# A contrast kernel: the first four tiles loaded through two queues, and the first store in one piece

## The chip, the cores and the metric

The kernel runs on one core of one Trainium2 chip. The metric is the time of one execution on the device in microseconds (us). Three runs of the kernel before gave 238.89, 239.13 and 239.41 us; the median, 239.13 us, is the time that the change is compared with.

## The reference

The input `x` is 16 x 3 images of 512 x 512 pixels in fp32, 50.33 MB, and the output has the same shape. Each image is pulled away from its own mean by a factor of 1.5 and clipped:

```python
mean = np.mean(x, axis=(2, 3), keepdims=True)
return np.clip(mean + factor * (x - mean), 0, 1).astype(np.float32)
```

## The kernel before

The input is taken as one flat array and cut into 12 tiles of 128 rows with 8192 numbers each: 32 KB in each of the 128 partitions, 4 MB a tile. An image fills 32 rows, so a tile holds four whole images, and each tile can be finished on its own.

The tiles pass through a ring of six buffers in SBUF (`BUFS = 6`); tile t lives in buffer t % 6 and is changed in place. The order is written out by hand in the last block of the function (L103 to L112): the loads of tiles 0 to 5 are issued at the start, then for each tile `compute(t)` runs, followed by the load of tile t + 6, which goes into the buffer that tile t leaves. That load can't be issued before tile t has been stored.

All loads (`load`, L68 to L76) go through SP's queue, which the profile calls q1. Tile 0 comes in two pieces, 2048 columns (`SHORT`) and then 6144; tile 1 comes whole; tiles 2 and 3 are one DMA, and so are tiles 4 and 5. All stores (`store`, L100 and L101) go through ScalarE's queue, q10 in the profile. A queue's DMAs are worked off in its own order, by 16 DMA engines that serve both queues.

For one tile, `compute` does the following. VectorE adds up the first 4352 columns (`SUM`) of each row (L81), while ScalarE adds up the other 3840 with an ACTIVATE (L84). TensorE multiplies the two columns of sums by a block matrix (L86, L87), which gives every row of an image the shift (1 - factor) x mean in PSUM. VectorE then computes factor x + shift (L91) and clips (L94), both over the whole tile in place, and ScalarE issues the store. For tile 0 alone the two steps L91 and L94 and the store are done in two parts (`FIRST`), 2048 columns and then 6144, so that the first store can be issued early.

ScalarE works in program order: a store that waits for L94 stands ahead of the ACTIVATE of the next tile.

Of the kernel before, what the change touches and what calls it, by code (L numbers as in the profile page):

```python
# [1 line left out]

# [4 lines left out]


P = 128  # L10
ROW = 8192
BUFS = 6
SHORT = 2048
FIRST = (SHORT, ROW - SHORT)
SUM = 4352


@with_exitstack
def kernel(
    ctx: ExitStack,  # L20
    tc: tile.TileContext,
    x: bass.AP,
    factor: float,
    out: bass.AP,
):

    nc = tc.nc
    f32 = mybir.dt.float32  # L30
    Alu = mybir.AluOpType
    Act = mybir.ActivationFunctionType

    B, C, H, W = x.shape
    n_img, n_pix = B * C, H * W
    ppi = n_pix // ROW
    per_tile = P // ppi
    n_tiles = n_img // per_tile
    assert ppi * ROW == n_pix and per_tile * n_tiles == n_img

    factor = float(factor)
    wconst = (1.0 - factor) / float(n_pix)

    x_f = x.rearrange("b c h w -> (b c h w)")
    out_f = out.rearrange("b c h w -> (b c h w)")

    def dram(ap, t, c0=0, c1=ROW):
        return bass.AP(tensor=ap.tensor, offset=t * P * ROW + c0, ap=[[ROW, P], [1, c1 - c0]])

    consts = ctx.enter_context(tc.tile_pool(name="consts", bufs=1))  # L50
    xpool = ctx.enter_context(tc.tile_pool(name="xpool", bufs=1))
    small = ctx.enter_context(tc.tile_pool(name="small", bufs=1))
    psum = ctx.enter_context(tc.tile_pool(name="psum", bufs=1, space=bass.MemoryType.PSUM))


    sums = small.tile([P, 2 * n_tiles], f32, name="sums")
    junk = small.tile([P, ROW - SUM], f32, name="junk")
    bias = psum.tile([P, n_tiles], f32, name="bias")

    blockw = consts.tile([P, P], f32, name="blockw")  # L60
    nc.gpsimd.memset(blockw, 0.0)  # L61
    for a in range(0, P, ppi):
        nc.gpsimd.memset(blockw[a : a + ppi, a : a + ppi], wconst)  # L63


    ring = xpool.tile([P, BUFS, ROW], f32, name="ring")

    def load(t, c0=0, c1=ROW, n=1):  # L68

        b = t % BUFS  # L70
        src = bass.AP(
            tensor=x_f.tensor,
            offset=t * P * ROW + c0,
            ap=[[ROW, P], [P * ROW, n], [1, c1 - c0]],
        )
        nc.sync.dma_start(out=ring[:, b : b + n, c0:c1], in_=src)  # L76

    def compute(t):
        xt = ring[:, t % BUFS, :]
        own = sums[:, 2 * t : 2 * t + 2]  # L80
        nc.vector.tensor_reduce(  # L81
            out=own[:, 0:1], in_=xt[:, 0:SUM], axis=mybir.AxisListType.X, op=Alu.add
        )
        nc.scalar.activation(out=junk, in_=xt[:, SUM:ROW], func=Act.Copy, accum_out=own[:, 1:2])  # L84
        shift = bias[:, t : t + 1]
        nc.tensor.matmul(shift, blockw, own[:, 1:2], start=True, stop=False)  # L86
        nc.tensor.matmul(shift, blockw, own[:, 0:1], start=False, stop=True)  # L87
        c = 0
        for n in FIRST if t == 0 else [ROW]:
            part = xt[:, c : c + n]  # L90
            nc.vector.tensor_scalar(  # L91
                out=part, in0=part, scalar1=factor, scalar2=shift, op0=Alu.mult, op1=Alu.add
            )
            nc.vector.tensor_scalar(  # L94
                out=part, in0=part, scalar1=0.0, scalar2=1.0, op0=Alu.max, op1=Alu.min
            )
            store(t, c, c + n)
            c += n

    def store(t, c0, c1):  # L100
        nc.scalar.dma_start(out=dram(out_f, t, c0, c1), in_=ring[:, t % BUFS, c0:c1])  # L101

    with tc.manual_schedule():  # L103
        load(0, c1=SHORT)
        load(0, c0=SHORT)
        load(1)
        load(2, n=2)
        load(4, n=2)
        for t in range(n_tiles):
            compute(t)  # L110
            if t + BUFS < n_tiles:
                load(t + BUFS)  # L112


# [1 line left out]
_INS = ['x', 'factor']  # L116
_OUTS = [((16, 3, 512, 512), 'float32')]

_NUMBERS = {'factor': 1.5}


# [26 lines left out]
```

## Time and profile before

| what | value |
|---|---|
| median of three runs | 239.13 us |
| span of the profiled execution, first to last instruction | 237.3 us |
| VectorE busy | 163.1 us in 38 instructions |
| ScalarE busy | 43.2 us in 25 instructions |
| TensorE busy | 14.1 us in 48 matmuls |
| bytes moved | 50.33 MB read, 50.33 MB written |

The span runs from the first to the last instruction of one profiled execution. No other time is recorded for that execution; the median of the unprofiled runs lies 1.8 us above its span. The strips of the page cut the span into 40 equal slices of 5.93 us; a digit is the busy share in tenths, 9 meaning nine tenths or more. In the list of groups, the numbers behind the first bar are the busy time and the mean duration in ns, and behind the second bar the idle time just before, with what ended it. The windows view gives the same for stretches that one chooses: busy time of each engine, the clock of TensorE, the share of the DMA engines and their rate in GB/s. In a timeline, the first two numbers are start and duration in us.

### The profile page before, as it was taken

Reading aid. Unit: us, or ns where it says so; the run is one execution under the profiler, and the core shown is the slowest. Engines: PE = TensorE matmul, PEld = TensorE weight load, DVE = VectorE, ACT = ScalarE, POOL = GpSimd, SP = SyncE. Lnnn points to the kernel's source line nnn. Section 1 sums busy time; section 2 is a strip of 40 time slices with the busy share of each in tenths; the row PEclk is TensorE's granted clock in tenths of the full one; section 3 lists DMA queues with packets and bytes.
Section 4 is the critical chain, followed back from the end, with each engine's and each line's share of the span. In section 5 each row is a group of like instructions: output and inputs, shape, how many; then the busy total and the mean of one; then the engine's idle time right before and its main releaser. Section 6 shows DMA issues by size and latency. Waiting matters only on the chain.

```text
span 237.3 us, 285 instructions
## 1 busy us (share of the span) xinstructions
PE 14.1 (6%) x48; PEld 12.0 (5%) x48; DVE 163.1 (69%) x38; ACT 43.2 (18%) x25; POOL 0.9 (0%) x9
## 2 busy tenths in 40 slices
PE   0010010001010001010010100100100100010000
PEld 0010010001010001010010100100100100010000
DVE  0079989048989328999989898891892795687000
ACT  2050230041050023050320504101400500500000
POOL 1000000000000000000000000000000000000000
DMA  7999999999999999999999999999999999999996
GB/s 297 410 442 442 421 442 359 456 439 441 442 436 414 403 431 442 442 442 442 436 442 436 414 409 425 442 442 442 442 436 442 436 420 403 425 442 442 442 442 265
DMA packets 3712, 100.66 MB, mean 424 GB/s; under 512 B 384, under 2 KB 384, under 8 KB 384
## 3 DMA queue, kind: packets, MB, share of 16 engines
q1 hardware_dynamic: 1840, 50.33, 49.7%
q10 hardware_dynamic: 1872, 50.33, 49.2%
HBM read 50.33 MB, written 50.33 MB: 424 GB/s over the span
## 4 chain that ended last, share of the span: by engine, by line
DMA 57%; DVE 29%; another core or an unknown queue 3%; PE 1%; SPq 1%; issue 0%; DVEq 0%
DMA ring<-in_x_dram 41%; DMA out_dram<-ring 16%; DVE sums L81 10%; DVE ring L91 9%; DVE ring L94 9%; PE bias L87 1%; SPq L76 1%; DVEq L91 0%
## 5 line engine op out<-in xcount | busy, mean ns | idle before, releaser
L81 DVE TENSOR_REDUCE sums<-ring 128x1 f32<-128x4352 f32 x12 | 56.2, 4683 | 45.7 <-DMA ring<-in_x_dram 45.7
L84 ACT ACTIVATE junk<-ring 128x3840 f32<-128x3840 f32 x12 | 40.8, 3403 | 163.3 <-DMA ring<-in_x_dram 107.5
L91 DVE TENSOR_SCALAR ring<-ring,bias 128x8192 f32<-128x8192 f32 (+2 forms) x13 | 54.1, 4163 | 8.9 <-PE bias L87 7.4
L94 DVE TENSOR_SCALAR ring<-ring 128x8192 f32<-128x8192 f32 (+2 forms) x13 | 53.3, 4099 | 0.4
L86 PE MATMUL bias<-sums,blockw 128*128 128x1 f32 x24 | 7.0, 361 | 190.8 <-ACT junk L84 190.8
L86 PEld LDWEIGHTS bias<-sums,blockw 128*128 128x128 f32 x24 | 6.0, 312 | 191.7 <-ACT junk L84 175.2
L87 PE MATMUL bias<-sums,blockw 128*128 128x1 f32 x24 | 7.0, 363 | 4.3 <-DVE sums L81 3.9
L87 PEld LDWEIGHTS bias<-sums,blockw 128*128 128x128 f32 x24 | 6.0, 311 | 5.3 <-DVE sums L81 5.0
L84 ACT ACTIVATION_READ_ACCUMULATOR junk<-ring 128x1 f32 x12 | 2.2, 186 | 0.0
L84 ACT ACT_TABLE_LOAD x1 | 1.3, 1283 | 0.7 <-PEq L129 0.7
L63 POOL MEMSET blockw<- 32x32 f32 x4 | 0.5, 117 | 0.2
L61 POOL MEMSET blockw<- 128x128 f32 x1 | 0.2, 204 | 0.3 <-POOLq L129 0.3
L129 POOL MEMSET const-bfloat16-1.0<- 128x1 bf16 x1 | 0.1, 111 | 0.0
L129 POOL MEMSET const-uint8-127<- 128x1 uint8 x1 | 0.1, 111 | 0.0
L129 POOL MEMSET const-float32-1.0<- 128x1 f32 x1 | 0.1, 108 | 0.0
L129 POOL MEMSET const-float32-0.0<- 128x1 f32 x1 | 0.1, 103 | 0.2 <-issue 0.2
## 6 DMA issues: line engine op xcount, KB each, us to landing
out_dram<-ring ACTq DMA_DIRECT2D x11, 4096.0 KB, 35.8
ring<-in_x_dram SPq DMA_DIRECT2D x7, 4096.0 KB, 49.7
ring<-in_x_dram SPq DMA_DIRECT2D x2, 8192.0 KB, 66.7
ring<-in_x_dram SPq DMA_DIRECT2D x1, 3072.0 KB, 11.7
out_dram<-ring ACTq DMA_DIRECT2D x1, 3072.0 KB, 28.2
ring<-in_x_dram SPq DMA_DIRECT2D x1, 1024.0 KB, 4.8
out_dram<-ring ACTq DMA_DIRECT2D x1, 1024.0 KB, 17.5
```

Of the source, the lines that this page charges most:

```text
L61: nc.gpsimd.memset(blockw, 0.0)
L63: nc.gpsimd.memset(blockw[a : a + ppi, a : a + ppi], wconst)
L76: nc.sync.dma_start(out=ring[:, b : b + n, c0:c1], in_=src)
L81: nc.vector.tensor_reduce(out=own[:, 0:1], in_=xt[:, 0:SUM], axis=mybir.AxisListType.X, op=Alu.add)
L84: nc.scalar.activation(out=junk, in_=xt[:, SUM:ROW], func=Act.Copy, accum_out=own[:, 1:2])
L86: nc.tensor.matmul(shift, blockw, own[:, 1:2], start=True, stop=False)
L87: nc.tensor.matmul(shift, blockw, own[:, 0:1], start=False, stop=True)
L91: nc.vector.tensor_scalar(out=part, in0=part, scalar1=factor, scalar2=shift, op0=Alu.mult, op1=Alu.add)
L94: nc.vector.tensor_scalar(out=part, in0=part, scalar1=0.0, scalar2=1.0, op0=Alu.max, op1=Alu.min)
L129: nc = _bacc.Bacc("TRN2", target_bir_lowering=False, num_devices=1)
```

## The change

The first four tiles are shared out between the two queues. SP's queue loads tile 0 (in two pieces, as before) and tile 2; ScalarE's queue loads tile 1, now in two pieces as well, and tile 3, and these three DMAs are issued ahead of everything else that ScalarE issues. Tiles 4 and 5 stay one DMA on SP's queue, and so do the later loads, one tile each. The stores stay on ScalarE's queue, behind those three loads. Tile 0 is no longer done in two parts: L91, L94 and the store take the whole tile, as for all others.

```diff
-FIRST = (SHORT, ROW - SHORT)
...
-    def load(t, c0=0, c1=ROW, n=1):
+    def load(t, c0=0, c1=ROW, n=1, queue=nc.sync):
...
-        nc.sync.dma_start(out=ring[:, b : b + n, c0:c1], in_=src)
+        queue.dma_start(out=ring[:, b : b + n, c0:c1], in_=src)
...
-        c = 0
-        for n in FIRST if t == 0 else [ROW]:
-            part = xt[:, c : c + n]
-            nc.vector.tensor_scalar(
-                out=part, in0=part, scalar1=factor, scalar2=shift, op0=Alu.mult, op1=Alu.add
-            )
-            nc.vector.tensor_scalar(
-                out=part, in0=part, scalar1=0.0, scalar2=1.0, op0=Alu.max, op1=Alu.min
-            )
-            store(t, c, c + n)
-            c += n
-
-    def store(t, c0, c1):
-        nc.scalar.dma_start(out=dram(out_f, t, c0, c1), in_=ring[:, t % BUFS, c0:c1])
+        nc.vector.tensor_scalar(
+            out=xt, in0=xt, scalar1=factor, scalar2=shift, op0=Alu.mult, op1=Alu.add
+        )
+        nc.vector.tensor_scalar(
+            out=xt, in0=xt, scalar1=0.0, scalar2=1.0, op0=Alu.max, op1=Alu.min
+        )
+        nc.scalar.dma_start(out=dram(out_f, t), in_=xt)
 
     with tc.manual_schedule():
         load(0, c1=SHORT)
+        load(1, c1=SHORT, queue=nc.scalar)
         load(0, c0=SHORT)
-        load(1)
-        load(2, n=2)
+        load(1, c0=SHORT, queue=nc.scalar)
+        load(2)
+        load(3, queue=nc.scalar)
         load(4, n=2)
         for t in range(n_tiles):
             compute(t)
```

## The prediction

> **What bounds the kernel now.** I read the page first for which resource is full, then the timeline of VectorE for the pace, then the windows for the places where that resource falls short of its own pace.
>
> ```profile
> span 237.3 us, 285 instructions
> ...
> DMA  7999999999999999999999999999999999999996
> GB/s 297 410 442 442 421 442 359 456 439 441 442 436 414 403 431 442 442 442 442 436 442 436 414 409 425 442 442 442 442 436 442 436 420 403 425 442 442 442 442 265
> ...
> q1 hardware_dynamic: 1840, 50.33, 49.7%
> q10 hardware_dynamic: 1872, 50.33, 49.2%
> HBM read 50.33 MB, written 50.33 MB: 424 GB/s over the span
> ...
> L81 DVE TENSOR_REDUCE sums<-ring 128x1 f32<-128x4352 f32 x12 | 56.2, 4683 | 45.7 <-DMA ring<-in_x_dram 45.7
> ```
>
> The DMA engines are at nine tenths or more in 38 of 40 slices: q1 (SP's loads) and q10 (ScalarE's stores) each carry 50.33 MB through the same 16 engines. VectorE, the busiest engine, waits 45.7 us for loads. The first and last slice are the unavoidable ends. The steady pace is the distance between two late tiles:
>
> ```profile
> 184.40 4.68 DVE L81 TENSOR_REDUCE sums<-ring 128x1 f32<-128x4352 f32 x1 [4.99 <-DMA ring<-in_x_dram]
> 189.82 4.49 DVE L91 TENSOR_SCALAR ring<-ring,bias 128x8192 f32<-128x8192 f32 x1 [0.74 <-PE bias L87]
> 194.35 4.43 DVE L94 TENSOR_SCALAR ring<-ring 128x8192 f32<-128x8192 f32 x1
> 203.76 4.69 DVE L81 TENSOR_REDUCE sums<-ring 128x1 f32<-128x4352 f32 x1 [4.98 <-DMA ring<-in_x_dram]
> ```
>
> 203.76 - 184.40 = 19.36 us, in which one tile is loaded and one stored: 8.389 MB / 19.36 us = 433 GB/s. VectorE needs 14.37 us of it (194.35 + 4.43 - 184.40 = 14.38). At 433 GB/s the 100.66 MB take 232.4 us. The trace's packets run from 1.74 to 236.06 us, that is 234.3 us: 1.9 us are lost in all, and the end (236.06 to 237.3) and the 1.8 us between the span and the median of the runs (239.13) lie outside the transfers. No other time of the profiled execution is recorded, so I carry changes of its span over to 239.13 one to one. Where the 1.9 us are:
>
> ```profile
> core 0: us, PE busy (x) PEld busy (x) DVE busy (x) ACT busy (x) POOL busy (x), PEclk, DMA share, GB/s
> 2.00:22.00 20.00, 1.15 (x4) 1.01 (x4) 8.33 (x4) 3.52 (x3) 0.00 (x0) 1.00 1.03 439
> 22.00:42.00 20.00, 1.18 (x4) 1.00 (x4) 19.08 (x5) 3.50 (x2) 0.00 (x0) 1.00 0.99 410
> 42.00:88.00 46.00, 2.35 (x8) 2.00 (x8) 27.54 (x7) 7.35 (x5) 0.00 (x0) 1.00 1.01 434
> ```
>
> The last number of a row is the rate. From 22 to 42 us it is 410: 20 x (1 - 410/433) = 1.06 us, of which the row before gives back 0.28 (439), since a packet is counted in one piece. So about **0.8 us** are lost where the stores begin. The packet records place it: a 32 KB row takes 1.213 us nearly always, but 1.26 to 1.51 around 24.0 to 26.1 (the first short store's first packets at 24.64), and 1.52 to 1.79 around 37.7 to 38.1 (between the short store's last packet at 36.9 and the long one's first at 38.3). Following the bytes against 433 GB/s gives the same: behind by 0.72 us up to 24 us (the ramp of the first load), by 1.0 at 32, by 1.55 at 46, and no further until the last packets; the rest is the spread of the 16 engines at the end (235.5 to 236.06).
>
> **The change part by part.**
>
> *Bytes and packets.* Nothing is removed: 100.66 MB stay. Split tiles: before, load 0 and store 0; after, loads 0 and 1. A split tile costs 128 x (0.309 + 0.912) / 16 - 128 x 1.213 / 16 = 9.77 - 9.70 = 0.06 us, one taken and one added: 0. There are 25 DMAs for 24; a further completion is 16 packets of 9 ns on 16 engines: 0.01 us. Expected packets: q1 128 + 128 + 9 x 128 + 10 x 16 = 1568, q10 128 + 128 + 13 x 128 + 15 x 16 = 2160, with 41.94 and 58.72 MB.
>
> A rule that speaks against one more short DMA: the Trainium skill, "SBUF — State Buffer", The DMA setup-cost knee, puts a fixed cost of about 2 us on every DMA and says to issue the largest possible; by it one more would make an estimated 241.1. The trace disagrees: 24 DMAs times 2 us would be 48 us, and all the loss is 1.9.
>
> *Issues.* SP's five first issues take 2.52 us together (L76, from 0.74). ScalarE gets three, about 0.4 us each by SP's single ones (0.37 to 0.42), beside a table load of 1.28; its first ACTIVATE waits until 12.88 anyway. They lie under the first load: 0. If the table load goes first, q10 starts some 1.3 us later, while q1 fills all engines alone: 0 too. On VectorE two instructions go: 1.29 + 1.23 + 3.42 + 3.36 = 9.30 us become 4.49 + 4.43 = 8.92; 0.4 us less on an engine that waits.
>
> *Order of transfers.* Here the change is large, and I follow it by hand, 19.4 us for 8.39 MB. Before, tiles 0 and 1 landed at 12.9 and 22.6. Now both queues load in turn, so both land near 22.6; VectorE starts some 9.6 us later. Store 0 is issued at 22.6 + 14.4 = 37.0 (before: 20.9 and 27.6). It stands behind load 3 in q10; loads 2 and 3 land near 42.0. Then load 4-5 (8.39 MB) goes beside stores 0 (lands 61.4) and 1 (80.8), issued at 37.0 and 51.3; after that load t+4 beside store t, one pair each 19.4 us: loads 6 to 11 land at 100.2, 119.6, 139.0, 158.4, 177.7, 197.1. Does either queue run dry? Load t+6 needs store t landed at 61.4 + 19.4 t and has its turn at 80.8 + 19.4 t: 19.4 us of cover. Store 2 is issued at 65.7 for a turn at 80.8, store 3 at 80.0 for 100.2, stores 4 to 7 at 95.2, 109.5, 123.8, 138.2 for 119.6, 139, 158.4, 177.7: 15 us of cover or more. The tightest is store 0, 37.0 for about 41; if that is late, q1 has load 4-5 and takes all engines, and nothing is lost but the order. The tail: tile 11 lands at 197.1 (before 203.7), its store is issued at 211.5, and stores 8, 9, 10 keep the engines until 226: 14.7 us of cover (before: 226.3 - 218.2 = 8.1). So the wait of VectorE moves from the late loads to the first 22 us, and the DMA engines stay full: **0**.
>
> *Ends of the phases.* What is left is the lost 0.8 us. The short store and the step from it to the long one go, and with them 0.27 + 0.52 us. In their place comes one hand-over from load 3 to store 0 near 41 us, on all 16 engines at once. From below: 0, as from the long store 0 to store 1 near 55 us, where no packet is longer than 1.235 us. From above: 0.8, all that both starts cost now. Nearest is the first start of a store, 0.27; I take 0.35. The ramp (0.72 us) may shrink with two queues (to no less than 0) or double with twice the short packets (0.72 more); the nearest row, one queue, leaves it as it is.
>
> Sum: -0.79 + 0.35 + 0.01 = -0.43 us: span about 236.8, median **238.7**.
>
> **The rivals.**
>
> *Two load streams slow each other* (slower). Tiles 0 and 1, then 2 and 3, are read at once, 4 MB apart; the trace has no such phase, only one load stream alone (439 in the row above) and load beside store (433). Place: 3 to 42 us. At 410, the lowest of these rows, 38.7 x (433/410 - 1) = 2.2 us minus the 0.4 gained: 240.9. It decides against me from about 422 GB/s (1.0 us lost, net +0.6). For it: the engines run in step then. Against it: load beside store ran at full pace in the same engines.
>
> The Trainium skill, "DMA: Bandwidth & Descriptors", Latency and other measured facts, reports that rows a power of two apart can alias in HBM: 103 GB/s at a pitch of 4 MiB against 214 in full. Halving the first 39 us would add an estimated 39 us (278); load 6 beside store 2, 16 MiB apart in two tensors, shows 433 here, and no run shows 4 MiB yet.
>
> *The hand-over loses as much as both store starts* (no gain): all 16 engines turn from load to store together, now with 32 KB packets on both sides. Net -0.1 to +0.4: 239.1 or a little above.
>
> *The ramp fills too*: two queues bring work to the engines sooner, no hand-over loss. -0.8 and up to 0.7 of the ramp: 238.0.
>
> *A late last tile* (slower): if stores got far more than half of the engines, load 11 would land late. It costs from a landing after 211.8; at worst, stores always first, 10 stores and 12 loads end at 3.2 + 22 x 9.69 = 216.4, that is 4.6 us: 243.3. The even pairs of before speak against it.
>
> *It doesn't do what it says*: were q10 to begin only after the first ACTIVATE, the first store would start as now, but whole, and only the 0.52 of the step to the long store would go: 238.6.
>
> **How the numbers follow.** A measurement of this kernel can tell about 0.2%, 0.48 us. Forecast (net -0.1 to -0.8, centre 238.7): 0.54, of it 0.25 beyond 0.48. No gain: 0.18, all within. Ramp too, or no loading from the start: 0.12, all faster. Load streams: 0.12, late tile 0.04, all slower. Faster 0.37, same 0.47, slower 0.16. The range leaves out the tail of the ramp case, most of the load-stream case and the late tile: 238.1 to 239.9.
>
> **What would show it.** Tile 0's L81 starts near 22.5; store 0 issues near 37; q1 1568 and q10 2160 packets; reductions 19.4 us apart from tile 6 on; the last L81 near 197; 433 GB/s from 3 to 40 us; the row from 22 to 42 us near 433; a dip after 41 of less than 0.5 us. I am wrong if the early rate is lower, if any slice in between falls under nine tenths, or if the last store is issued after 226.

## The result and the profile after

The changed kernel takes **242.88 us** (median of five runs, 242.72 to 243.42) against 239.13 (238.89 to 239.41): slower by 3.75 us, ratio 1.016 with a 95% interval of 1.0148 to 1.0173. The profiled execution itself took 243.42 us, 2.3 more than its span, and is the longest of the five. In the runs of the kernel before that stand beside the experiments, 1.9 us lie outside the span. So of the 3.75 us about 3.3 lie inside the span (240.6 us for the run of 242.88, against 237.3) and 0.4 outside it, where the profile shows nothing; the prediction carried the span over one to one and has no term for that.

The page of the changed kernel, its span, strips and queues:

```profile
span 241.1 us, 290 instructions
...
DMA  7999999999999999999999999999999999999992
GB/s 257 466 408 435 435 435 435 419 435 424 435 424 424 429 435 419 429 413 435 435 435 435 435 413 429 435 413 424 424 435 413 435 435 435 429 424 435 435 435 120
...
q10 hardware_dynamic: 2160, 58.72, 56.6%
q1 hardware_dynamic: 1568, 41.94, 41.3%
HBM read 50.33 MB, written 50.33 MB: 417 GB/s over the span
```

The bytes and packets are those worked out ahead, and the DMA engines are again nine tenths busy or more in every slice but the first and last. Yet the mean rate fell from 424 to 417 GB/s. So a full strip doesn't say at what pace the engines move. The pace shows in one long window of the steady part; first the changed kernel, then the kernel before (same columns as in the prediction, the last is GB/s):

```profile
90.00:195.00 105.00, 7.04 (x24) 6.01 (x24) 86.11 (x20) 20.98 (x12) 0.00 (x0) 1.00 1.00 427
```

```profile
90.00:195.00 105.00, 8.21 (x28) 7.01 (x28) 88.76 (x21) 22.11 (x14) 0.00 (x0) 1.00 1.01 434
```

427 against 434 over 105 us is 1.7 us. VectorE's timeline of the changed kernel shows the same from the other end:

```profile
141.34 4.68 DVE L80 TENSOR_REDUCE sums<-ring 128x1 f32<-128x4352 f32 x1 [3.64 <-DMA ring<-in_x_dram]
160.87 4.69 DVE L80 TENSOR_REDUCE sums<-ring 128x1 f32<-128x4352 f32 x1 [5.15 <-DMA ring<-in_x_dram]
180.66 4.68 DVE L80 TENSOR_REDUCE sums<-ring 128x1 f32<-128x4352 f32 x1 [5.42 <-DMA ring<-in_x_dram]
200.22 4.69 DVE L80 TENSOR_REDUCE sums<-ring 128x1 f32<-128x4352 f32 x1 [5.19 <-DMA ring<-in_x_dram]
```

Tiles come 19.53, 19.79 and 19.56 us apart, not 19.36. The rest of the loss is at the end. The DMA view of the last 5 us of transfers, cut into 40 pieces of 0.125 us, first the changed kernel (236 to 241 us), then the one before (232 to 237):

```profile
DMA  9900660006660006000060000000000000000000
DMA packets 27, 0.36 MB, mean 72 GB/s; under 512 B 16, under 2 KB 16, under 8 KB 16
```

```profile
DMA  9066000099906600009990900000000000000000
DMA packets 55, 1.28 MB, mean 256 GB/s; under 512 B 16, under 2 KB 16, under 8 KB 16
```

In these views a packet appears at one moment, so read how many there are. Before, all 16 engines carry on until their last rows, which end within 0.6 us. In the changed kernel, from 236 us on only 11 rows of 32 KB (0.36 MB) are left, and they trickle out over 3.8 us. Each DMA counts 16 completions, one per engine; the last store's come from 236.57 to 240.13 us, with a median of 237.14. Before they come from 235.84 to 236.44, median 235.96. So the 3.7 us by which the last transfer of this execution ends later split into **1.2 us by which the middle engine is later, and 2.5 more by which the slowest engine is behind the middle one** (3.0 against 0.5).

Where is the pace lost? A packet is what a DMA moves for one row of a tile. In the packet records of 90 to 195 us, a row of 32 KB takes 1.213 us as a rule. Those that take over 1.25 us, from here on the late packets, number 0 of 1392 before and 114 of 1368 after; the longest takes 2.95 us. They cluster where DMAs end: in the changed kernel a load ends near 99.4, 118.9, 138.4, 157.8 and 177.6 us, a store 2.4 us later each time, and 96 of the 114 lie from 4 us before to 5 us after such a store's end; 88 of the 114 are rows of loads. Before, loads end at 105.3, 124.7 and 144.0 us and stores half a tile away from them.

### The profile page after: what moved, and what is told of

It reads as the page before. It is cut to its first block, busy times and chain, and to the rows that moved or that the text cites. A ratio compares the mean times of both kernels' runs of the same rounds, so it can differ in the third digit from the quotient of the medians.

```text
span 241.1 us, 290 instructions
## 1 busy us (share of the span) xinstructions
PE 14.1 (6%) x48; PEld 12.0 (5%) x48; DVE 162.7 (67%) x36; ACT 43.2 (18%) x25; POOL 0.9 (0%) x9
## 4 chain that ended last, share of the span: by engine, by line
DMA 44%; DVE 28%; another core or an unknown queue 8%; ACT 3%; PE 2%; issue 2%; ACTq 0%; SPq 0%; DVEq 0%
DMA ring<-in_x_dram 24%; DMA out_dram<-ring 20%; DVE ring L87 11%; DVE ring L90 11%; DVE sums L80 6%; ACT junk L83 3%; PE bias L86 1%; PE bias L85 1%; ACTq L93 0%; SPq L75 0%; DVEq L87 0%; ACTq L83 0%; DVEq L80 0%
## 5 line engine op out<-in xcount | busy, mean ns | idle before, releaser
L87 DVE TENSOR_SCALAR ring<-ring,bias 128x8192 f32<-128x8192 f32 x12 | 53.9, 4492 | 9.0 <-PE bias L86 7.5
L90 DVE TENSOR_SCALAR ring<-ring 128x8192 f32<-128x8192 f32 x12 | 53.1, 4427 | 0.4
```

The source lines that it names most:

```text
L87: nc.vector.tensor_scalar(out=xt, in0=xt, scalar1=factor, scalar2=shift, op0=Alu.mult, op1=Alu.add)
L90: nc.vector.tensor_scalar(out=xt, in0=xt, scalar1=0.0, scalar2=1.0, op0=Alu.max, op1=Alu.min)
```

## The experiments

All time ratios are against the kernel before, run on the same chip. The distance is the time from the end of a load to the end of the nearest store, each taken as the median of its 16 completions. Theory A: time is lost at every such pair of ends when the distance has a certain size. Its rivals: B, the whole first store; C, loads on ScalarE's queue in themselves; D, row addresses of load and store that go in step.

**One part at a time.** `whole_store_only` is the kernel before with

```diff
-FIRST = (SHORT, ROW - SHORT)
+FIRST = (ROW,)
```

> One part alone: all loads on SP's queue as before, but the first store in one piece. Theory A (DMA ends in step: an engine loses time when its load queue and its store queue both pass from one DMA to the next within a packet or two): store 0 is issued near 27.4, its first packets come near 31, when the load of tiles 2 and 3 is 7 to 8 of its 16 packets per engine along; so the ends of loads and stores would fall about one packet apart and the time be 241 to 243, or 238.6 if they miss each other by two or more. Theory B (the whole first store is the cause): 242.9. Theory C (loads on ScalarE's queue are the cause in themselves): 238.6 to 239.1.

Measured 241.41 (1.0096, 1.0081 to 1.0111). `two_queues_only` is the changed kernel with the loop over `FIRST` and `store` put back.

> The other part alone: the first four tiles on both queues as in the changed kernel, but the first store in two pieces as before. Both pieces have 8 packets per engine, so they keep step with the tiles of load 4-5. Theory A: as the changed kernel, 242 to 243.5, with late packets where loads and stores end together. Theory B: 239.1 to 239.6. Theory C: 242.9.

Measured 240.65 (1.0063, 1.0048 to 1.0078). Neither B nor C holds: each part alone loses, and neither as much as both. The two losses, 2.3 and 1.5 us, do add up to the whole, but they are other losses than that of the changed kernel, and `shift1` below, which has both parts, has neither. Few late packets show in them: 23 and 5 between 90 and 195 us. The whole store alone loses 1.15 us near 31 us, where the stores begin (0.83 before), and ends with its slowest engine 1.9 us behind the median; its 241.41 lies in the range that theory A gave, but by luck, since its ends lie 0.3 us apart and not one packet. With two queues and a split store, the short store's 8 KB packets alternate with 32 KB rows, so load 4-5 lands at 70.4 and not 80.0 us; load 6 has to wait for store 0 (71.4), SP's queue runs dry, and 0.85 us are lost between 80 and 90 us. My expectation for this run, equal packet counts that keep step, missed that. Theory A needed a direct test.

**Shift the queues against each other.** `shift1`, `shift2`, `shift4`, `shift6` and `shift8` are the changed kernel with a useless load of SHIFT x 16 rows of 256 bytes, which has SHIFT packets on each engine. It moves 4 to 33 KB but takes that many turns between the queues:

```diff
+SHIFT = 1
...
+    pad = small.tile([16 * SHIFT, 64], f32, name="pad")
...
         load(3, queue=nc.scalar)
+        nc.scalar.dma_start(
+            out=pad, in_=bass.AP(tensor=x_f.tensor, offset=0, ap=[[ROW, 16 * SHIFT], [1, 64]])
+        )
```

> The changed kernel with a useless load of 64 rows of 256 bytes (4 packets per engine) on ScalarE's queue between load 3 and store 0. It costs under 0.1 us of transfers and puts the stores 4 packets, half a tile, behind the loads. Theory A: the losses at the common ends go, including part of the one near 41 us: 238.6 to 239.6, engines within 1 us of each other at the end. Theories B and C: 242.9 as the changed kernel.

> The same useless load with 128 rows: 8 packets per engine, as many as a whole tile, so loads and stores end together again. Theory A: 242 to 243.5. If any further DMA between loads and stores helps whatever its count: 238.6 to 239.6. Theories B and C: 242.9.

Measured: `shift4` 239.59 (1.0019, 1.0010 to 1.0029), `shift8` 241.00 (1.0082, 1.0064 to 1.0100). The first came as theory A said, except that the loss where the stores begin didn't shrink (0.9 us, against 0.7 in the changed kernel). The second is slow for another reason: SP's queue ran dry near 72 us as in `two_queues_only`, after which the ends lay 9.5 us apart and no packet was late. So it never came to the distance that it was meant for.

> The changed kernel with a useless load of 16 rows, 1 packet per engine, between load 3 and store 0. In the changed kernel a store ends 2.4 us after a load, one packet of each queue; with 4 such packets it was 14.2 us and with 8 the queues began 1.2 us apart. Theory A (late packets come again and again where a store ends one packet after a load): the stores end 4.8 to 7.3 us after the loads, only the loss at the start of the stores (0.7 to 1.2 us) is left: 239.4 to 240.3. Theory D (the row addresses of load and store go in step): one or two rows further apart, still in step: 241 to 243.

> The same with 2 packets per engine: the stores end 7 to 10 us after the loads. Theory A: 239.4 to 240.3. Theory D: 241 to 243.

> The same with 6 packets per engine: the stores end some 2 to 4 us ahead of the loads. If only the order load, then store costs: 239.4 to 240.7. If nearness costs in either order: 241 to 243.

Measured: `shift1` **239.30** (1.0005, 0.9995 to 1.0015), `shift2` 239.63 (1.0015, 1.0005 to 1.0024), `shift6` 239.77 (1.0036, 1.0021 to 1.0050). One packet of 256 bytes per engine takes back 3.6 of the 3.75 us. Inside its span, `shift1` is even 0.2 us shorter than the kernel before (237.1 against 237.3); outside it lie 2.2 us for 1.9. The steady window of `shift1`:

```profile
90.00:195.00 105.00, 7.04 (x24) 6.02 (x24) 86.70 (x20) 22.11 (x13) 0.00 (x0) 1.00 1.01 434
```

The pace is 434 again. `shift6` didn't reach the distance that I wanted: it ran dry like `shift8`.

**The addresses.** `rows_moved` is the changed kernel with

```diff
-        nc.scalar.dma_start(out=dram(out_f, t), in_=xt)
+        n = P if t < n_tiles - 1 else P - 16
+        dst = bass.AP(tensor=out_f.tensor, offset=(t * P + 4) * ROW, ap=[[ROW, n], [1, ROW]])
+        nc.scalar.dma_start(out=dst, in_=xt[:n])
```

> The changed kernel with every store written 4 rows (128 KB) further on in the output, and tile 11 stored without its last 16 rows, which takes 0.52 MB or 1.2 us off the end; the order of the DMAs and their ends stay. Theory A: the late packets stay, 241.7. Theory D: they go, 238.2 to 239.5.

Measured 245.08 (without the longest of its four runs 1.0228, 1.0194 to 1.0261). Its times scatter (243.74 to 248.53), and the profiled execution is the longest, so I read only its pattern: ends 2.4 us apart and 111 late packets in the same clusters. Even its fastest run lies 4 us above D's range. Moving the addresses in the output by 128 KB doesn't take the loss away; D in that form falls. In SBUF the rows that load and store touch stay in step in this run, so that form of D isn't tested by it; that the late packets gather round the ends of DMAs (105 of the 111) speaks against it. Why this kernel is slower still than the changed one is open.

**Bring the loss into the kernel before.** `before_shift4` and `before_shift5` are the kernel before with the useless load behind store 0:

```diff
             compute(t)
+            if t == 0:
+                nc.scalar.dma_start(
+                    out=pad, in_=bass.AP(tensor=x_f.tensor, offset=0, ap=[[ROW, 16 * SHIFT], [1, 64]])
+                )
```

> The kernel before with a useless load of 64 rows of 256 bytes (4 packets per engine) on ScalarE's queue behind the second piece of store 0. In the kernel before the stores end 9 to 10 us from the loads; this puts them 4 to 5 packet slots of 2.4 us later, to 0 to 2.4 us behind a load's end. Theory A (a store that ends about one packet after a load costs time at each such end): 240.5 to 243 with late packets every 19.4 us, if the ends meet that distance. If the loss of the changed kernel belongs to its own start and not to the distance: 239.1 to 239.6.

> The same with 5 packets per engine: 2.4 to 4.8 us behind a load's end. Theory A: 240.5 to 243 where the distance is near 2.4, 239.1 to 239.8 where it is 4.8. Otherwise: 239.1 to 239.6. The two runs together cover the distance of the changed kernel.

Measured: `before_shift4` 239.43 (1.0010, 1.0001 to 1.0019), `before_shift5` **248.41** (1.0401, 1.0363 to 1.0439). With 4 packets the ends fall together (0.2 us) and nothing happens; with 5 the stores end 2.4 us behind the loads, and the kernel loses 9.2 us, far beyond what I expected. One more packet per engine makes the difference. The window and two tiles of `before_shift5`:

```profile
90.00:195.00 105.00, 7.03 (x24) 6.01 (x24) 81.78 (x19) 20.99 (x12) 0.00 (x0) 1.00 1.00 422
```

```profile
144.48 4.69 DVE L84 TENSOR_REDUCE sums<-ring 128x1 f32<-128x4352 f32 x1 [5.59 <-DMA ring<-in_x_dram]
165.72 4.69 DVE L84 TENSOR_REDUCE sums<-ring 128x1 f32<-128x4352 f32 x1 [6.87 <-DMA ring<-in_x_dram]
```

The DMA share is 1.00 and the rate 422; these two tiles come 21.2 us apart, the next ones 20.5 and 19.9. In this kernel, too, some engines fall further and further behind: the spread of a load's 16 completions grows from 1.7 us (load 4-5) over 2.8, 4.6, 6.3, 8.1 and 9.0 to 9.5 (load 11). Each tile's VectorE work waits for the slowest.

The loss isn't the same in kind, though. In the changed kernel the late packets are mostly loads and lie near the ends. Here 123 of the 211 are stores, only 127 lie in the same stretch about the ends, and three engines carry most of the lag (5.5, 6.7 and 8.1 us behind the median at load 11). The distance sets it off, but the 9.2 us are not simply the changed kernel's loss once more.

**The other order.** `sp_shift1`, `sp_shift2` and `sp_shift3` have the useless load on SP's queue, between loads 2 and 4-5, so that the loads are put back:

> The changed kernel with the one-packet useless load on SP's queue instead, between load 2 and load 4-5, so that the loads and not the stores are put back. On ScalarE's queue one packet moved the ends by 4.8 us (2.4 to 7.2); here the stores should end from 0 to 2.4 us ahead of the loads. If only a store that ends one packet behind a load is dear, the late packets of every 19.4 us go: 239.2 to 240.2. If one packet apart is dear in either order and the distance comes out at 2.4: 241 to 248.

> As the run before, with 2 packets per engine on SP's queue: one packet there moved the ends by 2.6 us (from 2.4 behind to 0.2 ahead), so the stores should end some 2.6 to 2.8 us ahead of the loads, one packet apart in the other order. If only a store one packet behind a load is dear: 239.4 to 240.4, no late packets every 19.4 us. If one packet apart is dear in either order: 241 to 248 with such packets.

> With 3 packets per engine: the stores end some 5 us ahead of the loads, two packets apart. Both theories: 239.4 to 240.4, as in the run with 14.2 us (5.2 ahead), 239.6.

Measured: 240.17 (1.0038, 1.0024 to 1.0051), 240.01 (1.0034, 1.0020 to 1.0049) and 240.00 (1.0034, 1.0021 to 1.0047), with stores 0.2, 2.4 and 4.9 us ahead of the loads and 5, 0 and 1 late packets. One packet apart is not dear as such; it is the store that ends one packet behind the load. That these three are still 0.7 to 1.0 us above the kernel before is in part a larger loss where the stores begin, 1.05 to 1.15 us near 41 us for 0.83, and in part the 0.4 us more outside the span.

All runs together, by the distance in the steady part (negative: the store ends first). Distance, late packets and the spread of the last store's 16 completions are those of the profiled execution; in `shift6` and `rows_moved` that is the longest of its kernel:

```
kernel             distance us  late packets  last store, slowest - first  median us
shift8             -9.5           0           0.93                         241.00
two_queues_only    -8.4           5           0.95                         240.65
sp_shift3          -4.9           1           0.47                         240.00
shift4             -4.9           0           0.49                         239.59
sp_shift2          -2.4           0           0.52                         240.01
sp_shift1          -0.2           5           0.48                         240.17
before_shift4       0.2           5           0.34                         239.43
whole_store_only    0.3          23           2.14                         241.41
after               2.4         114           3.56                         242.88
before_shift5       2.4         211           8.16                         248.41
rows_moved          2.4         111           9.41                         245.08
shift1              7.2           0           0.55                         239.30
before              9.6           0           0.60                         239.13
shift2              9.6           0           0.46                         239.63
rows_to_scalar      9.6           0           2.39                         254.11
shift6              9.7           0           1.41                         239.77
```

`shift8`, `two_queues_only` and `shift6` ran dry on SP's queue, and `rows_to_scalar` follows below; their times have other causes. Between 2.4 and 7.2 us no run lies, so where the dear stretch of distances ends is open.

**A repair without a useless transfer** failed. `rows_to_scalar` moves the last 16 rows of tile 2 to ScalarE's queue:

```diff
-        load(2)
+        rows = P - 16
+        src = 2 * P * ROW
+        nc.sync.dma_start(
+            out=ring[:rows, 2, :], in_=bass.AP(tensor=x_f.tensor, offset=src, ap=[[ROW, rows], [1, ROW]])
+        )
         load(3, queue=nc.scalar)
+        nc.scalar.dma_start(
+            out=ring[rows:, 2, :],
+            in_=bass.AP(tensor=x_f.tensor, offset=src + rows * ROW, ap=[[ROW, P - rows], [1, ROW]]),
+        )
```

> A repair without a useless transfer: the changed kernel, with the last 16 rows of tile 2 (one packet per engine) moved from SP's queue to ScalarE's, behind load 3. That sets the queues two packets apart, as the single useless packet did: stores end near 7 us behind the loads. Theory A: 239.0 to 239.7. If it takes a small transfer ahead of the first store to repair it: 241 to 243.

Measured 254.11 (1.0600, 1.0573 to 1.0627). Three windows of it, the first while the load of 112 rows is under way, the second with the load of 16 rows:

```profile
22.00:47.00 25.00, 2.32 (x8) 2.00 (x8) 22.25 (x5) 6.99 (x4) 0.00 (x0) 1.00 1.00 280
47.00:60.00 13.00, 0.00 (x0) 0.00 (x0) 4.87 (x2) 0.00 (x0) 0.00 (x0) 1.00 0.98 252
60.00:195.00 135.00, 10.55 (x36) 9.01 (x36) 114.31 (x26) 31.48 (x18) 0.00 (x0) 1.00 1.00 433
```

The shift itself worked: from 60 us on the pace is 433, with ends 9.6 us apart (7 expected). But while the two parts of the divided tile are under way, all DMAs together move only 280 and 252 GB/s: rows of 32 KB take 1.4 to 2.3 us beside the load of 112 rows, in both queues, and up to 4.1 us beside the load of 16. No kernel tried beats the one before; `shift1` equals it.

## Why the prediction was wrong

**The step that failed** is the order of transfers, "load t+4 beside store t, one pair each 19.4 us", priced at 0 because neither queue runs dry. Neither did, and the hand schedule held: the first reduction began at 22.83 us (22.5 foretold), store 0 was issued at 37.25 (37.0), the loads of tiles 4-5 and 6 were complete at 80.4 and, in the middle engine, 99.4 (80.8, 100.2), and the last store was issued at 214.6, well ahead of its turn at 226. None of the three signs that the prediction named for being wrong showed. I treated 16 engines and two queues as one pipe with a rate. What that left out is where the DMAs of the two queues end against each other. In the changed kernel the loads of both queues end together near 42 us, 0.2 us apart. From the next pair of ends on (80.0 and 82.4 us) the stores end 2.4 us behind the loads, and since both queues then have equal tiles, the distance stays. The runs show that this distance is the cause: one further packet per engine takes the loss away, five put a loss into the kernel before, and four do not. Why the store must be behind, and by one packet, is not shown.

In numbers, by the bytes moved against 433 GB/s: the ramp cost 0.87 us (0.72 before; I had left it as it is), the start of the stores 0.70 (0.83 before; I had 0.35), and between 80 us and the end of the loads 1.6 us went that I had at 0. That makes 1.6 us more than before, averaged over the engines. The other 2.1 is the slowest engine behind the average. **That term was missing altogether**: chained end to start, the packet records make 16 series, one for each engine, of 6.28 to 6.30 MB each in both kernels. So an engine that had lost time got none of its work taken over and ended last. From the median engine, the same 3.7 us read 1.2 and 2.5, as above. These sums are those of the profiled execution and end with its last transfer; the 0.4 us outside the span come on top.

**The hand-over near 41 us** was there, in its place, and twice my 0.35; in the runs with `shift` in their names that come from the changed kernel it came at 0.5 to 1.2. So the forecast gain of 0.43 wouldn't have come without the dear distance either: `shift1`, which hasn't got it, is at 239.30, within 0.1% of before. About half of the gain is there in its span (0.2 us), and the longer stretch outside the span takes it away.

**The rivals.** The load streams don't slow each other: between 4 and 40 us the bytes fall only 0.1 us behind 433 GB/s. The row-pitch figures that the prediction weighed (Trainium skill, "DMA: Bandwidth & Descriptors", Latency and other measured facts) are for the pitch between the rows of one copy; two loads of contiguous rows, 4 MiB apart, show nothing of the kind here. The last tile did come late (200.2 for 197.1), through the slowest engine and not through an uneven share of the queues, and stayed under its 211.8, so it cost nothing. Slower had a chance of 0.16, all on these two, and none on what happened; the range ended at 239.9.

**One more short DMA** costs nothing that shows, as I had it by the row: `shift1` has two more than the kernel before and is within 0.2 us of it. The fixed 2 us that the Trainium skill puts on every DMA ("SBUF — State Buffer", The DMA setup-cost knee) don't add up for DMAs that stand in a queue: in `shift1`, with 26 of them, the transfers fall 1.4 us behind 433 GB/s in all.

The Trainium skill says in "DMA: Bandwidth & Descriptors", Issuing engines are not separate DMA queues, that issuing DMAs from several engines only saves issue time, since all of them interleave on the same DMA engines. The traces agree on the interleaving (rows of q1 and q10 take turns). But the queue counts too, by which DMA ends beside which: the same DMA of one packet per engine took the changed kernel from 242.88 to 239.30 on ScalarE's queue and to 240.17 on SP's.

## What to carry to other kernels

When the DMA engines are full, "full" is not yet a rate: compare GB/s over a long window with the best pace that the same profile shows, and compare the 16 completions of one DMA, since the slowest engine sets the end. Two full queues with equal DMAs kept the distance of their ends to the end of the kernel here, and one distance (a store's end about one packet behind a load's) cost up to 1.6% in one kernel and set off a loss of 4% in another. It is cheap to test: a useless DMA of a few small rows on one queue shifts the ends, and if the time moves by far more than those bytes and no queue has run dry, the distance matters.

## What the runs showed of the hardware that was not expected

- Late packets came in numbers only where a store's last packet follows a load's last by one turn: 114 and 211 of some 1360 in two kernels with 2.4 us, at most 5 from -9.5 to -0.2 and from 7.2 us up; at 0.2 to 0.3 us 5 in one kernel, 23 in another.
- An engine that had fallen behind stayed behind: in `before_shift5` the spread of a load's completions grew with every load from tiles 4-5 on, from 1.7 to 9.5 us, while the median engine lost 2 us in the whole run.
- A tile divided into loads of 112 and 16 rows ran at 280 and 252 GB/s together with its neighbours, against 433 for loads of 128 rows, with the DMA engines busy all the time (shares of 1.00 and 0.98). Whether it is the count or the rows' place is open.
- Where the stores begin beside running loads, 0.5 to 1.2 us are lost once, in every kernel in which that can be told apart, around the first store's first packets or its end. Why is open.
